# PEER gather on one Trainium2 core: remaining u dots and the first v-row gathers issued at the last u tile, v rows at a new pace

## The chip, the cores and the metric

The kernel runs on 1 core of one Trainium2 chip. The metric is device time in microseconds (us) of one execution. Before the change the median of 3 runs is 1949.45 us (1948.42 to 1951.34).

## What is computed

Two decoder layers over 256 tokens with 1024 channels, then a final RMS norm. Each layer is a token mixer (attention) and then PEER, a feed-forward layer that looks up experts. The change touches PEER alone. Per token it does this, for 8 heads with 16 chosen experts each out of 16384:

```python
q = (ht @ wq).reshape(PEER_CHUNK, PEER_HEADS, 2, half)
...
act = jax.nn.gelu(jnp.einsum('td,thkd->thk', ht, u[e]))
return jnp.einsum('thk,thkd->td', gate * act, v[e])
```

`e` are the numbers of the chosen experts (top-k of two half keys), `gate` a softmax over their scores. `u` and `v` are tables of 16384 rows of 1024 float32 values (64 MB each) per layer.

## The kernel before

The 256 tokens of a layer are split. The first ND = 160 tokens are computed **densely**: `u` is walked in NI = 128 tiles of 128 experts, each tile multiplied with all 160 tokens (L1444), put through GELU on ScalarE (L1432) and kept in SBUF as `A` (128 experts x 160 tokens per tile). The gates are then spread into `A` by one-hot products, and `v` is walked in 128 tiles of 128 rows that are multiplied with `A` and summed in four PSUM banks (L1506). The other 96 tokens (`PARTS`: 64 tokens with 2 slots each, 32 with 4) are computed by **gathering**: GpSimd issues indirect DMAs (L1215) that fetch 128 rows of `u` or `v` each, one row per partition, 96 for `u` and 96 for `v` per layer (`LOTS`). A gather of u rows is used by one dot on VectorE (`dot`, L1236); when all 96 dots are there, ScalarE applies GELU to them (`weigh`, L1240) and VectorE multiplies the gates in (`gated`, L1243). A gather of v rows is used by one scaled addition on VectorE (`axpy`, L1250 and L1252; two sums, `side` for the 64 tokens, `rows` for the 32).

The stages of a layer's PEER, on TensorE (PE): query products; 128 u tiles (L1420 to L1445); the one-hot stage of 40 steps of four tokens (`tb`, L1456 to L1475), where GpSimd makes one and VectorE three of four one-hots (L1409), ScalarE the other side (L1398, L1404), PE the gate products (`spread_gates`, L1416) and VectorE multiplies them into `A` (L1475); 128 v tiles (L1498 to L1522). Four tiles before the end, `gathered_part` (L1485) folds the two sums of gathered rows into the tokens by products with a stacking matrix: first half `side` (L1491, 128x64), second half `rows` (L1491, 128x32). The last three v tiles follow it on PE.

What sets the order. The program is written in one order by the Python loops, and every engine works through its own part of it in that order. A gather needs a free room (1024 columns): five in `side`, two in `rows`, and three more (`htok`, `junk`) once `gated` is issued. `pump()` issues gathers for the rooms that are free; `step(n)` calls it, uses row set n and gives its room back. `gather()` takes the next of the generator's steps (dots, `weigh`, `gated`, additions) if it may run, and the credit says how many steps a tile issues: 0.8 per u tile (`FETCH_PACE`), and per v tile `V_PACE` = (0.7 up to tile 106, then 1.2):

```python
credit[0] = min(credit[0] + V_PACE[0 if i < V_PACE[1] else 2], 2.0)
if credit[0] > 0 and head(gathers) is not None and i < NI - 9:
    nc.vector.tensor_copy(seen, ahead[max(ahead)][:, 0:1])
while credit[0] > 0 and gather():
    credit[0] -= 1
```

The `seen` copy (L1510) makes VectorE wait for the newest v tile that has been asked for before the steps of the tile run, so that the next gather goes out only after it. At tile 122 (`NI - GE`) all steps that are left are issued. The v tiles are loaded from SP's queue (`feed`, L387) into ten pieces (the first twelve at step 2 of the one-hot stage: six pieces, four places in `flat`, two in `spare`), gathers go over GpSimd's queue. In layer 0 the next layer's first weights are loaded at tile 119 (L1560) and split at tiles 122, 125 and 126 (`CUTS`, L395 on ScalarE, L397 on VectorE).

Of the kernel before, what the change touches and what calls it, by code (L numbers as in the profile page):

```python
# [28 lines left out]
NI = 128  # L29
# [29 lines left out]
GP = 4  # L59
HAND = 9  # L60
CUTS = {NI - 6: 1, NI - 3: 2, NI - 2: 3}
V_PACE = (0.7, 106, 1.2)
BG = (1, 0.7)
N0 = 2
C01 = 0
# [51 lines left out]
class Build:  # L117
# [1080 lines left out]
    def gather_steps(self, l, Q, more):  # L1198

        nc = self.nc  # L1200
        col = lambda i: Q[:, 1024 * i:1024 * (i + 1)]
        free = [col(i) for i in (0, 1, 2, 3, 7)] + more[2:]
        junk = col(6)
        htok, acc = [col(4), more[0]], [col(5), more[1]]
        dots = self.dots
        box = []

        open_to = lambda n: n < len(todo) and todo[n][3] <= self.rows

        def pump():  # L1210
            n = len(box)
            while free and open_to(n):
                table, lot = todo[n][0], todo[n][1]
                r = free.pop(0)
                nc.gpsimd.indirect_dma_start(out=r, out_offset=None, in_=self.a[table],  # L1215
                                             in_offset=bass.IndirectOffsetOnAxis(ap=self.gidx[:, lot:lot + 1], axis=0))
                box.append(r)
                n += 1

        starts = [SEQ - sum(n for n, _ in PARTS[:a + 1]) for a in range(len(PARTS))]  # L1220

        def join(a):
            n, per = PARTS[a]
            h2 = junk.rearrange("p (k s t) -> p k s t", k=KC, s=per)
            for k in range(KC):
                nc.vector.tensor_copy(h2[:, k], self.whole[:, k, None, starts[a]:starts[a] + n].to_broadcast([128, per, n]))

        def tokens(a, half):
            p = self.bank()
            for j in range(4):  # L1230
                k = 4 * half + j
                nc.tensor.transpose(p[:, j * 128:(j + 1) * 128], junk[:, k * 128:(k + 1) * 128], self.ident)  # L1232
            nc.scalar.activation(htok[a][:, half * 512:half * 512 + 512], p, AF.Copy)

        def dot(n, lot, a):
            nc.vector.scalar_tensor_tensor(junk, box[n], 1.0, htok[a], op0=OP.mult, op1=OP.mult,  # L1236
                                           accum_out=dots[:, lot:lot + 1])

        def weigh():
            nc.scalar.activation(dots, dots, AF.Gelu_apprx_tanh)  # L1240

        def gated():
            nc.vector.tensor_mul(dots, dots, self.ggate)  # L1243

        begun = set()

        def axpy(n, lot, a):
            if a not in begun:
                begun.add(a)
                nc.vector.tensor_scalar(acc[a], box[n], dots[:, lot:lot + 1], None, op0=OP.mult)  # L1250
            else:
                nc.vector.scalar_tensor_tensor(acc[a], box[n], dots[:, lot:lot + 1], acc[a], op0=OP.mult, op1=OP.add)  # L1252

        lots = []
        for heads in (4, 8):
            at = 0
            for a, (n, per) in enumerate(PARTS):
                w = 64 // per
                lots += [(at + (heads // 4 - 1) * w + i, a, heads) for i in range(w)]
                at += 128 // per  # L1260
        todo = [("u", lot, dot, heads, a) for lot, a, heads in lots] + [("v", lot, axpy, 8, a) for lot, a, heads in lots]

        def step(n):
            pump()
            todo[n][2](n, todo[n][1], todo[n][4])
            free.append(box[n])

        self.gacc = acc
        self.pump = pump
        for a in range(len(PARTS)):  # L1270
            for f in (lambda a=a: join(a), lambda a=a: tokens(a, 0), lambda a=a: tokens(a, 1)):
                yield (lambda: True), f
        for n in range(len(todo)):
            if n == LOTS:
                yield (lambda: self.routed[1]), weigh
                yield (lambda: self.routed[1]), gated
                free += [*htok, junk]
            yield (lambda n=n: n < len(box) or bool(free) and open_to(n)), lambda n=n: step(n)

    def peer(self, l, want, pos, early, then):  # L1280
# [12 lines left out]
        gathers = iter(())  # L1293
        self.pump = lambda: None
        heads = {}
        credit = [0.0]
        self.tv = self.tp = self.now = 0.0
        self.rows = self.q_done = 0
        self.asked, self.routed, self.coded = [False, False], [False, False], [False, False]
        END = (0.0, None, None)  # L1300

        def head(x):
            if x not in heads:
                heads[x] = next(x, None)
            return heads[x]
# [17 lines left out]
        def finish():  # L1323
            while route(True):
                pass
            assert all(self.routed)

        def gather():
            s = head(gathers)
            if s is None or not s[0]():  # L1330
                return False
            del heads[gathers]
            self.dve(1.2)
            s[1]()
            return True

        def fill(pace, most):
            if self.rows:
                credit[0] = min(credit[0] + pace, 3.0)
            while self.tv < self.now + most:  # L1340
                if credit[0] > 0 and gather():
                    credit[0] -= 1
                elif not route():
                    break
# [30 lines left out]
        gathers = self.gather_steps(l, G, [more[n // 2][:, n % 2] for n in range(4)])  # L1375
# [44 lines left out]
        for i in range(NI + 1):  # L1420
            if i == NI - 1:
                diffs = [self.bank() for _ in range(ND_)]
                for n in range(ND_):
                    differences(n)
            if i == NI:
                ohs = [self.piece(F32).rearrange("p (a n) -> p a n", a=8) for _ in range(NOH)]
                gates = [self.bank() for _ in range(NGB)]
                begin(0)
                begin(1)
                oh = [one_hots(n, False) for n in range(2)]  # L1430
            if i:
                nc.scalar.activation(dst(i - 1), ps.pop(i - 1)[:, :ND], AF.Gelu_apprx_tanh)  # L1432
            if i < NI:
                self.now += T_U
                if i == QROW:
                    finish()
                w = v(want(u0 + i, most=DEEP))
                for n, (b, after) in tiles.items():
                    if after >= 0 and after + 1 == i:
                        early[u0 + n] = ring[b]  # L1440
                        nc.sync.dma_start(ring[b], self.a["uT"][l, n])
                p = ps[i] = self.bank()
                for k in range(KC):
                    nc.tensor.matmul(p[:, :ND], w[:, k], self.whole[:, k, :ND], start=(k == 0), stop=(k == KC - 1))  # L1444
                fill(FETCH_PACE[0], SLACK)  # L1445
            else:
                first = spread_gates(0)
        vsrc = [self.a["v"][(l * NI + i) * 128:(l * NI + i + 1) * 128] for i in range(NI)]
# [7 lines left out]
        for tb in range(nb):  # L1456
# [5 lines left out]
            if tb == 2:  # L1462
                want(0, -1, most=PIECES - NOH)
                for n in range(4):
                    i = PIECES - NOH + n
                    ahead[i] = flat[:, NI * ND + n * UNIT:NI * ND + (n + 1) * UNIT]
                    nc.sync.dma_start(ahead[i], vsrc[i])
                for n in range(2):
                    i = PIECES - NOH + 4 + n
# [28 lines left out]
        for i in range(NI):  # L1498
            if i == NI - HAND:
                then([*[flat[:, NI * ND + n * UNIT:][:, :UNIT] for n in range(4)],  # L1500
                      *[spare[:, n * UNIT:(n + 1) * UNIT] for n in range(2)]])
            if l + 1 < DEPTH and i in CUTS:
                self.next[0](0, CUTS[i], most=0)
            r = want(i, most=DEEP if i < NI - 8 else 4)
            for k in range(KC):
                nc.tensor.matmul(acc[k], r[:, k * 128:(k + 1) * 128], dst(i), start=i == 0 and k % 2 == 0, stop=i == NI - 1,  # L1506
                                 skip_group_check=True)
            credit[0] = min(credit[0] + V_PACE[0 if i < V_PACE[1] else 2], 2.0)
            if credit[0] > 0 and head(gathers) is not None and i < NI - 9:
                nc.vector.tensor_copy(seen, ahead[max(ahead)][:, 0:1])  # L1510
            while credit[0] > 0 and gather():
                credit[0] -= 1
            if i == NI - GE:
                while gather():
                    pass
            if i == NI - GP:
                gathered_part()
            if i == NI - 2:
                for k in range(KC):
                    self.sum_chunk(squares[:, k], ND, SEQ, k)  # L1520
            if i == NI - SQ:
                self.load_sqrt()  # L1522
# [137 lines left out]
```

## Time and profile before

| | |
|---|---|
| median of 3 runs | 1949.45 us (1948.42 to 1951.34) |
| the profiled execution | 1956.64 us, its span 1954.8 us |
| TensorE (PE) busy | 1857.3 us, 95% |
| weight loads (PEld) | 1779.2 us, 91% |
| VectorE (DVE) | 1288.4 us, 66% |
| ScalarE (ACT) | 500.4 us, 26% |
| GpSimd (POOL) | 573.4 us, 29% |
| DMA | 605.26 MB, mean 310 GB/s; SP's queue 401.71 MB, GpSimd's 201.35 MB |
| granted TensorE clock, mean | 0.971 of full speed |

The profile is of one execution, a few us longer than the median of the runs. An engine's share is an average over stages with different limits, so the stages are read one by one: by the groups of instructions (what ended the idle time ahead of them), by the timeline of an engine in a stretch, and by the busy time and traffic of stretches. [...]

### The profile page before, as it was taken

How to read it: one execution, taken by the hardware profiler on the slowest of the kernel's cores; microseconds unless marked ns; L12 is line 12 of the kernel's file. 1: busy time of each engine (PE TensorE's matmuls, PEld its weight loads, DVE VectorE, ACT ScalarE, POOL GpSimd, SP SyncE). 2: the span in 40 equal slices, each digit the busy share in tenths (PEclk: the TensorE clock that was granted, in tenths of full speed). 3: DMA queues.
4: the chain of work that ended last, by engine and by line, in shares of the span. 5: the costliest groups of instructions: out<-in, count | busy, mean ns of one | idle time of the engine just before them, and what ended most of it. 6: DMA issues, size and time to landing. Idle time of an engine off the chain costs nothing. (4 is left out here: it accounts for less than half of the span.)

```text
span 1954.8 us, 34450 instructions
## 1 busy us (share of the span) xinstructions
PE 1857.3 (95%) x13284; PEld 1779.2 (91%) x13284; DVE 1288.4 (66%) x3084; ACT 500.4 (26%) x1079; POOL 573.4 (29%) x524
## 2 busy tenths in 40 slices
PE   5899999999999999999879999999999999999996
PEld 4778898999999899999868799899999998999995
DVE  8788765789854854444765987578995458344456
ACT  3444545211211710000025554522111154000001
POOL 4000005245443533322400000243454344322341
PEclk7899999999999999999989999999999999999997
DMA  7767656899999379999926574589999974999993
GB/s 274 282 229 261 218 162 240 325 386 365 409 408 409 140 270 375 409 409 408 407 96 240 204 267 163 200 294 366 366 409 408 409 295 145 349 408 408 407 410 155
DMA packets 166484, 605.26 MB, mean 310 GB/s; under 512 B 18480, under 2 KB 19120, under 8 KB 166192
## 3 DMA queue, kind: packets, MB, share of 16 engines
q1 hardware_dynamic: 111024, 401.71, 54.8%
q0 software_dynamic: 55296, 201.35, 26.3%
q8 instruction: 105, 1.72, 0.4%
q14 instruction: 59, 0.48, 0.1%
HBM read 601.94 MB, written 1.05 MB: 308 GB/s over the span
## 5 line engine op out<-in xcount | busy, mean ns | idle before, releaser
L1506 PE MATMUL bank<-wide,piece 128*128 128x160 f32 x3904 | 535.8, 300 | 2.6 <-DVE wide L1475 2.6
L1506 PEld LDWEIGHTS bank<-wide,piece 128*128 128x128 f32 x3904 | 534.4, 191 | 3.0 <-DVE wide L1475 3.0
L1444 PE MATMUL bank<-whole,piece 128*128 128x160 f32 x2624 | 360.7, 299 | 0.7 <-issue 0.4
L1444 PEld LDWEIGHTS bank<-whole,piece 128*128 128x128 f32 x2624 | 357.5, 190 | 1.6 <-issue 1.6
L1215 POOL DMA_INDIRECT side<-in_u_dram,routes x140 | 164.1, 1172 | 263.5 <-DVE side L1236 161.6
L397 POOL TENSOR_TENSOR piece<-piece 128x1024 fp32r<-128x1024 f32 x28 | 68.2, 2442 | 530.3 <-ACT piece L395 526.9
L1510 DVE COPY seen<-piece 128x1 f32<-128x1 f32 x176 | 27.0, 153 | 294.1 <-DMA piece<-in_v_dram 285.8
L1215 POOL DMA_INDIRECT side<-in_v_dram,routes x134 | 135.3, 1010 | 281.2 <-DVE side L1252 170.1
L1444 PE MATMUL bank<-whole,wide 128*128 128x160 f32 x1472 | 205.5, 299 | 3.1 <-issue 3.1
L1444 PEld LDWEIGHTS bank<-whole,wide 128*128 128x128 f32 x1472 | 201.3, 190 | 3.6 <-issue 3.4
L1432 ACT ACTIVATE wide<-bank 128x160 f32<-128x160 f32 x256 | 77.7, 305 | 469.3 <-PE bank L1444 406.0
L420 PE MATMUL bank<-hHL,piece 128*128 128x256 f32 (+1 forms) x592 | 176.7, 299 | 17.5 <-ACT hHL L344 14.2
L421 PE MATMUL bank<-hHL,piece 128*128 128x256 f32 (+1 forms) x592 | 174.9, 295 | 5.5 <-POOL hHL L347 4.3
L422 PE MATMUL bank<-hHL,piece 128*128 128x256 f32 (+1 forms) x592 | 173.5, 293 | 4.5 <-DVE piece L397 3.4
L395 ACT ACTIVATE piece<-piece 128x1024 fp32r<-128x1024 f32 x140 | 146.3, 1062 | 98.6 <-issue 37.3
L397 DVE TENSOR_TENSOR piece<-piece 128x1024 fp32r<-128x1024 f32 (+1 forms) x112 | 138.3, 1240 | 49.5 <-ACT piece L395 43.3
L1236 DVE SCALAR_TENSOR_TENSOR side<-side 128x1024 f32<-128x1024 f32 x94 | 114.9, 1222 | 45.0 <-DMA side<-in_u_dram,routes 35.1
L420 PEld LDWEIGHTS bank<-hHL,piece 128*128 128x128 f32 (+1 forms) x592 | 117.5, 199 | 20.4 <-ACT hHL L344 15.1
L421 PEld LDWEIGHTS bank<-hHL,piece 128*128 128x128 f32 (+1 forms) x592 | 117.2, 198 | 9.4 <-POOL hHL L347 6.4
L422 PEld LDWEIGHTS bank<-hHL,piece 128*128 128x128 f32 (+1 forms) x592 | 117.5, 199 | 6.5 <-DVE piece L397 4.9
L1252 DVE SCALAR_TENSOR_TENSOR side<-side,routes 128x1024 f32<-128x1024 f32 x86 | 110.5, 1285 | 0.4 <-DMA side<-in_v_dram,routes 0.3
L261 DVE SCALAR_TENSOR_TENSOR wide<-wide 128x1024 f32<-128x1024 f32 x80 | 97.7, 1222 | 16.9 <-DMA wide<-in_w_ada_dram 16.9
(244 smaller groups left out, 2777.8 us busy)
## 6 DMA issues: line engine op xcount, KB each, us to landing
piece<-in_v_dram SPq DMA_DIRECT2D x244, 512.0 KB
piece<-in_uT_dram SPq DMA_DIRECT2D x164, 512.0 KB
piece<-in_W_dram SPq DMA_DIRECT2D x147, 512.0 KB
wide<-in_uT_dram SPq DMA_DIRECT2D x92, 512.0 KB
wide<-in_w_ada_dram SPq DMA_DIRECT2D x80, 512.0 KB
side<-in_w_ada_dram SPq DMA_DIRECT2D x16, 512.0 KB
wide<-in_v_dram SPq DMA_DIRECT2D x8, 512.0 KB
side<-in_u_dram,routes POOLq DMA_INDIRECT x140
```

The lines of the kernel that those rows point to most:

```text
L261: nc.vector.scalar_tensor_tensor(buf(n), buf(n), 1.0, self.S["silu"], op0=OP.mult, op1=OP.mult, accum_out=self.mod[l][:, u:u + 1])
L395: nc.scalar.activation(Hs[i], raws[i], AF.Copy)
L397: self.subs.append(lambda: eng.tensor_sub(Ls[i], raws[i], Hs[i].bitcast(F32)))
L420: mm(out, l[0], r[0], start=start, stop=False, skip_group_check=True)
L421: mm(out, l[0], r[1], start=False, stop=False, skip_group_check=True)
L422: mm(out, l[1], r[0], start=False, stop=stop, skip_group_check=True)
L1215: nc.gpsimd.indirect_dma_start(out=r, out_offset=None, in_=self.a[table], in_offset=bass.IndirectOffsetOnAxis(ap=self.gidx[:, lot:lot + 1] ...
L1236: nc.vector.scalar_tensor_tensor(junk, box[n], 1.0, htok[a], op0=OP.mult, op1=OP.mult, accum_out=dots[:, lot:lot + 1])
L1252: nc.vector.scalar_tensor_tensor(acc[a], box[n], dots[:, lot:lot + 1], acc[a], op0=OP.mult, op1=OP.add)
L1432: nc.scalar.activation(dst(i - 1), ps.pop(i - 1)[:, :ND], AF.Gelu_apprx_tanh)
L1444: nc.tensor.matmul(p[:, :ND], w[:, k], self.whole[:, k, :ND], start=(k == 0), stop=(k == KC - 1))
L1506: nc.tensor.matmul(acc[k], r[:, k * 128:(k + 1) * 128], dst(i), start=i == 0 and k % 2 == 0, stop=i == NI - 1, skip_group_check=True)
```

## The change

Three things. At the last u tile (`i == NI - 1`) all dots that are left, `weigh` and `gated` are issued, and then `pump()` is called, so that v rows are gathered into every free room ahead of the one-hot stage (`self.weighed` counts the two steps). `V_PACE` becomes (1.25 for 8 tiles, then 0.74). The `seen` copy is left out in the first 8 v tiles.

```diff
-V_PACE = (0.7, 106, 1.2)
+V_PACE = (1.25, 8, 0.74)
...
         def weigh():
             nc.scalar.activation(dots, dots, AF.Gelu_apprx_tanh)
+            self.weighed = 1
 
         def gated():
             nc.vector.tensor_mul(dots, dots, self.ggate)
+            self.weighed = 2
...
-        self.rows = self.q_done = 0
+        self.rows = self.q_done = self.weighed = 0
...
                 fill(FETCH_PACE[0], SLACK)
+                if i == NI - 1:
+                    while self.weighed < 2 and gather():
+                        pass
+                    head(gathers)
+                    self.pump()
...
-            if credit[0] > 0 and head(gathers) is not None and i < NI - 9:
+            if credit[0] > 0 and head(gathers) is not None and V_PACE[1] <= i < NI - 9:
                 nc.vector.tensor_copy(seen, ahead[max(ahead)][:, 0:1])
```

How it moves instructions, at three places (both layers have the same). Line numbers behind the change are higher: its L1411 is L1409 of before (a one-hot), L1482 is L1475, L1244 is L1243 (`gated`), L1254 is L1252 (an addition), L1489 is L1482 (the tokens' sums).

GpSimd, from the last gathers of u rows to the first gathers of the v stage, as a difference (`piece` is a one-hot, `side` and `rows` the rooms):

```order
 L1215 DMA side<-in_u_dram,routes 128x1024 x5
-L1215 DMA rows<-in_v_dram,routes 128x1024
-L1409 TENSOR_SCALAR piece<-cst,routes 128x128 x5
-L1215 DMA rows<-in_v_dram,routes 128x1024
-L1409 TENSOR_SCALAR piece<-cst,routes 128x128 x35
+L1215 DMA rows<-in_v_dram,routes 128x1024 x2
 L1215 DMA side<-in_v_dram,routes 128x1024 x6
 L1215 DMA rows<-in_v_dram,routes 128x1024
 L1215 DMA side<-in_v_dram,routes 128x1024
+L1411 TENSOR_SCALAR piece<-cst,routes 128x128 x40
```

Ten gathers of v rows stand ahead of the 40 one-hots, where one stood ahead of them and one behind the fifth.

VectorE at the end of the u stage of layer 0. Before:

```order
L1236 SCALAR_TENSOR_TENSOR side,routes<-side,rows 128x1024 x5
L1236 SCALAR_TENSOR_TENSOR side,routes<-rows 128x1024 x2
L1409 TENSOR_SCALAR piece<-cst,routes 128x128 x9
L1475 TENSOR_TENSOR wide<-wide,bank 128x128x4
```

With the change:

```order
L1236 SCALAR_TENSOR_TENSOR side,routes<-side,rows 128x1024 x5
L1236 SCALAR_TENSOR_TENSOR side,routes<-rows 128x1024 x2
L1236 SCALAR_TENSOR_TENSOR side,routes<-side,rows 128x1024 x5
L1244 TENSOR_TENSOR routes<-routes 128x96
L1411 TENSOR_SCALAR piece<-cst,routes 128x128 x9
L1482 TENSOR_TENSOR wide<-wide,bank 128x128x4
```

Five dots and `gated` stand ahead of the first nine one-hots; before, they stood among the first v tiles.

VectorE at the end of the v stage of layer 0, from the last `seen` copy. Before:

```order
L1510 COPY seen<-piece 128x1
L1252 SCALAR_TENSOR_TENSOR rows<-side,routes,rows 128x1024 x5
L397 TENSOR_TENSOR piece<-wide,piece 128x1024 x2
L1252 SCALAR_TENSOR_TENSOR rows<-side,routes,rows 128x1024
L1252 SCALAR_TENSOR_TENSOR rows<-rows,routes 128x1024
L1252 SCALAR_TENSOR_TENSOR rows<-side,routes,rows 128x1024
L1252 SCALAR_TENSOR_TENSOR rows<-rows,routes 128x1024 x2
L1252 SCALAR_TENSOR_TENSOR rows<-side,routes,rows 128x1024 x4
L1482 SCALAR_TENSOR_TENSOR xT<-bank,mod_75,xT 128x64 x8
```

With the change:

```order
L1517 COPY seen<-piece 128x1
L1254 SCALAR_TENSOR_TENSOR rows<-rows,routes 128x1024
L1254 SCALAR_TENSOR_TENSOR rows<-side,routes,rows 128x1024 x3
L397 TENSOR_TENSOR piece<-wide,piece 128x1024 x2
L1254 SCALAR_TENSOR_TENSOR rows<-side,routes,rows 128x1024
L1489 SCALAR_TENSOR_TENSOR xT<-bank,mod_75,xT 128x64 x8
```

Five additions stand behind the last `seen` copy where fourteen stood, one of them behind the splits of the next layer's weights, where nine stood. In layer 1 there are no splits, and five and fourteen additions.

## Rows read from the trace of the kernel before

**Rows 1.** The page, busy time, share of the span and instructions of an engine.

```profile
PE 1857.3 (95%) x13284; PEld 1779.2 (91%) x13284; DVE 1288.4 (66%) x3084; ACT 500.4 (26%) x1079; POOL 573.4 (29%) x524
```

**Rows 2.** Groups by shape: count | busy us, mean ns | idle before, releaser.

```profile
L1506 PE MATMUL bank<-wide,piece 128*128 128x160 f32 x3904 | 535.8, 300 | 2.6 <-DVE wide L1475 2.6
...
L1491 PE MATMUL bank<-cst,rows 128*128 128x32 f32 x32 | 7.2, 401 | 27.5 <-DVE rows L1252 27.5
```

**Rows 3.** PE's timeline, layer 0's v stage: start us, us, what [idle before].

```profile
718.40 4.51 PE L1506 MATMUL bank<-wide,whole 128*128 128x160 f32 x32
...
968.33 1.89 PE L1491 MATMUL bank<-cst,side 128*128 128x64 f32 x16
986.49 3.60 PE L1491 MATMUL bank<-cst,rows 128*128 128x32 f32 x16 [16.27 <-DVE rows L1252]
989.90 6.55 PE L1506 MATMUL bank<-wide,piece 128*128 128x160 f32 x32
```

**Rows 4.** PE's timeline, the end of layer 1's v stage.

```profile
1915.76 1.89 PE L1491 MATMUL bank<-cst,side 128*128 128x64 f32 x16
1928.85 3.60 PE L1491 MATMUL bank<-cst,rows 128*128 128x32 f32 x16 [11.19 <-DVE rows L1252]
1932.26 6.42 PE L1506 MATMUL bank<-wide,piece 128*128 128x160 f32 x32
```

**Rows 5.** Stretches: us, busy of PE, PEld, DVE, ACT, POOL; PEclk, DMA, GB/s.

```profile
660.00:680.00 20.00, 20.00 (x133) 17.57 (x133) 20.00 (x59) 16.44 (x30) 12.38 (x15) 1.00 0.00 1
...
850.00:900.00 50.00, 50.00 (x370) 50.00 (x369) 22.11 (x33) 0.00 (x0) 15.03 (x16) 1.00 1.03 409
...
950.00:970.00 20.00, 20.00 (x153) 20.00 (x151) 14.38 (x17) 2.12 (x2) 11.29 (x10) 1.00 1.03 409
970.00:990.00 20.00, 3.73 (x19) 3.62 (x18) 15.53 (x20) 0.00 (x0) 1.02 (x1) 0.59 0.64 252
```

**Rows 6.** VectorE's timeline, the ends of the v stages of layers 0 and 1.

```profile
961.01 0.15 DVE L1510 COPY seen<-piece 128x1 f32<-128x1 f32 x1 [1.16 <-issue]
...
963.57 0.15 DVE L1510 COPY seen<-piece 128x1 f32<-128x1 f32 x1 [1.17 <-DMA piece<-in_v_dram]
963.68 6.57 DVE L1252 SCALAR_TENSOR_TENSOR rows<-side,routes,rows 128x1024 f32<-128x1024 f32 x5
970.16 2.36 DVE L397 TENSOR_TENSOR piece<-wide,piece 128x1024 fp32r<-128x1024 f32 x2
...
985.06 1.28 DVE L1252 SCALAR_TENSOR_TENSOR rows<-side,routes,rows 128x1024 f32<-128x1024 f32 x1 [0.28 <-DMA side<-in_v_dram,routes]
...
1910.24 7.89 DVE L1252 SCALAR_TENSOR_TENSOR rows<-side,routes,rows 128x1024 f32<-128x1024 f32 x6
```

**Rows 7.** Stretches, additions of line 1252 alone: us, DVE busy (count); PEclk, DMA, GB/s.

```profile
697.00:760.00 63.00, 15.42 (x12) 1.00 0.93 342
...
697.00:970.00 273.00, 108.93 (x85) 1.00 1.00 392
```

**Rows 8.** Timelines around layer 0's last u tile: VectorE, ScalarE, PE, GpSimd.

```profile
621.27 1.23 DVE L1236 SCALAR_TENSOR_TENSOR side<-rows 128x1024 f32<-128x1024 f32 x1 [1.33 <-DMA rows<-in_u_dram,routes]
...
622.42 1.75 DVE L1409 TENSOR_SCALAR piece<-cst,routes 128x128 f32<-128x128 f32 x6
...
643.72 0.69 DVE L1475 TENSOR_TENSOR wide<-wide,bank 128x512 f32<-128x512 f32 x1 [17.74 <-PE bank L1416]
...
638.67 0.30 ACT L1432 ACTIVATE wide<-bank 128x160 f32<-128x160 f32 x1 [2.25 <-PE bank L1444]
...
710.54 0.28 ACT L1240 ACTIVATE routes<-routes 128x96 f32<-128x96 f32 x1 [19.09 <-DVE side L1236]
...
642.56 1.05 PE L1416 MATMUL bank<-piece 128*128 128x128 f32 x8
...
643.04 0.79 POOL L1409 TENSOR_SCALAR piece<-cst,routes 128x128 f32<-128x128 f32 x1 [15.04 <-PE bank L1416]
```

**Rows 9.** SP's loads by line, 690 to 1000 us: count, ns min/median/max, first and last start.

```profile
L387 SPq DMA_DIRECT2D piece<-in_v_dram x116: 327/328/430, 691.3 to 966.1; - x116
```

## The prediction

> **What bounds the kernel now.** I read the page first: TensorE (PE) is busy 95% of the span [rows 1], so time can only come from the stretches where it stands still or runs at the lower clock. The groups of instructions by shape tell where those are. The products with the v tiles (L1506) have 2.6 us of idle time ahead of 3,904 records, but the second half of `gathered_part` (L1491 with `rows` as input) has 27.5 us ahead of its 32, released by the adding up of gathered v rows on VectorE (L1252) [rows 2]. That is the largest wait of PE for another engine in either layer's FFN, and the timeline of PE puts it in two places. In layer 0 PE ends the first half at 970.22 (968.33 + 1.89) and starts the second at 986.49: 16.27 us idle [rows 3]. In layer 1 it ends at 1917.65 and starts at 1928.85: 11.19 us [rows 4].
>
> The wait has a tail. After it, 16 records of the second half take 3.60 us where the 16 of the first took 1.89, and two v tiles take 6.55 us, where two at full clock take 4.51 [rows 3]; in layer 1 they take 3.60 and 6.42 [rows 4]. [...] So a stall costs its own length and then 1.71 + 2.04 us in layer 0, and 1.71 + 1.91 us in layer 1.
>
> Why the rows are late. VectorE's timeline shows it differently in each layer. In layer 1, fourteen row additions run back to back from the last `seen` copy: 6 take 7.89 us, so 14 take 18.4, from 1910.24 to 1928.7 [rows 6]. In layer 0, fourteen are left from 963.68, with two splits of the next layer's weights (2.36 us) among them, and the last addition waits until 985.06 for its gather to land [rows 6]. Behind both stand the transfers. A v tile and a gather are 512 KB each, which is 1.28 us at the 409 GB/s of 850 to 900 [rows 5]. On PE the 115 v tiles from tile 10 (718.40) to the first half of `gathered_part` (968.33) take 2.173 us each [rows 3]. At 0.7 gathers per tile the queues want 1.7 x 1.28 = 2.18 us per tile, all there is; the late pace of 1.2 wants 2.82. And two idle stretches are never made up: 660 to 680, in the one-hot stage, moves 1 GB/s [rows 5], and 697 to 760 moves 342 GB/s with 12 row additions done [rows 7], so (1 - 342/409) x 63 = 10.3 us of transfer time are lost there.
>
> **The change, part by part** (per layer, layer 0's times).
>
> *The last five dots, early.* VectorE ends its dots at 622.5 and then stands idle for 17.74 us before its first gate product at 643.72 [rows 8]. Dots come 2.56 us apart, paced by landings (1.23 us of work and 1.33 us of waiting [rows 8]). Five more end near 622.5 + 5 x 2.56 = 635.3. They are moved, not added: at their old place, the head of the v stage, no PE work waited for them. Cost 0, covered by VectorE's idle time; without that cover they would cost 5 x 1.3 = 6.5 us per layer.
>
> *Weighing ahead of the one-hots.* It stands on ScalarE behind the activation at 638.67 and takes 0.28 us [rows 8], so it ends near 639.3; `gated` follows to about 639.8. Behind it on VectorE wait nine one-hots that ran from 622.4: 1.75 us for 6 [rows 8], so 2.6 us for all, to 642.4. PE's first gate product at 642.56 [rows 8] needs only the first three of them (640.7), and the first product on VectorE was at 643.72. On ScalarE the step before the one-hots moves by 0.3 us at most. Cost 0 to 1.
>
> *Gathers ahead of GpSimd's one-hots.* GpSimd now issues ten v gathers before its first one-hot, where it issued one, then five one-hots, then another. Six go out while the dots run; four follow the last dot at about 0.95 + 0.3 us each, so GpSimd is free near 635.5 + 5 = 640.5 and its one-hot (0.79 us [rows 8]) is done before 642.56. The other bound is that each of the four waits for a landing at the shared rate, 4 x 2.56 = 10.2 us. I take 0.5 us per layer for the head as a whole: the rows around it show 17 us of slack, and it is nearest to those.
>
> *Eight gathers moved into the idle stretch.* Ten v gathers instead of two are issued before the gate products. The twelve v tiles loaded there plus eight gathers are 26 us of transfers, and 660 to 680 has next to none [rows 5]. Free for PE: no product needs them before 696. In the v stage 116 tile loads [rows 9] and 94 gathers become 116 and 86: 202 x 1.28 = 259 us instead of 269, against 125 tiles x 2.173 + 1.9 = 273.5 us of PE to the point where the rows must be ready.
>
> *Ten additions without a `seen` copy, then 0.74.* At 1.25 per tile for eight tiles ten additions run on VectorE at once (13 us), freeing ten rooms by about 710. The 10.3 us lost before 760 are recovered in part or in full. At 0.74 the queues want 1.74 x 1.28 = 2.23 us per tile, 0.057 more than PE takes: 5.9 us of lag over tiles 8 to 111. There the gathers end (the 96th goes out when the 86th addition frees its room) and the last 11 tiles want only 1.28 us each, so the lag is made up.
>
> *The end.* Layer 1 now has five additions behind the last `seen`: even if that copy came as late as now, 1910.2 + 5 x 1.31 = 1916.8, before the 1917.65 at which PE gets there. Residue 0. In layer 0 four additions, the two splits and one addition stand there: 963.7 + 5.3 + 2.4 + 1.3 = 972.7 at worst by that route, and by landings 985.06 - 10.3 = 974.8 with nothing of the lost time recovered, 964.5 with all, plus 1.3; PE arrives at 970.22. Residue 0 to 5.9 us; I take 1.5, nearer the recovered end because ten rooms come free at once.
>
> **Sum.** Waits 16.27 + 11.19 = 27.5; low clock 3.75 + 3.62 = 7.4; together 34.8. Given back: 1.5 in layer 0, 1.0 at the two heads. Net 32.3 us: the profiled execution would go from 1956.64 to 1924.3. Its time is 7.2 us over the median of the runs, 1949.45. If that difference stays, the median becomes 1917; if all of it lay in these waits, 1924. I take **1918 us**.
>
> Where the freed time goes next: PE runs through both halves and the last three tiles at full clock. The next thing that could be late is the squares of the gathered tokens, wanted two tiles (4.4 us) after the second half, and ready 2.3 us after it (1.36 us on VectorE, 0.85 on ScalarE). They fit.
>
> **A rule against the change.** The additions at the end of layer 0 come 2.56 us apart, each behind the `seen` copy of a new v tile (961.01, 963.57 [rows 6]): a v tile lands every 2.56 us, twice its 1.28 us, while both queues have work. [...]
>
> **The rivals.**
> *Rows still late.* The 5.9 us of lag and the next layer's weights on the same queue eat what was won. For it: 0.74 is over what the queues give. Against: 10.3 us are moved away for certain, and layer 1's end hangs on VectorE's 14 additions, not on landings. Half of the 34.8 stays: gain 17.4, 1932 (1922 to 1938). Chance 0.12.
> *The one-hot stage starts late.* GpSimd's four gathers wait for landings, 10.2 us per layer: 20.4 of the 34.8 back, net 14, 1935. For it: the twelve v tiles load at that time. Against: at most ten transfers stand ahead and VectorE has 17 us of slack. Chance 0.06.
> *It does not do what it says.* The `seen` copies hold the additions to the landing of tiles from tile 8 on, so the earlier start is lost by the end and the same stall returns: 1946 to 1953. Against: fewer additions are left behind the last copy whatever the copies do. Chance 0.05.
> *Slower: v tiles late.* With ten rooms free at once the gathers keep their queue full and a v tile lands every 2.56 us against 2.173 on PE. Eight tiles ahead are 17.4 us of cover; at 0.387 us per tile it is gone after 45 tiles in a row, and that is the point from which it decides. Over tiles 8 to 111 PE would wait 40 - 17.4 = 22.6 us per layer, 45 in all, less the 32 gained: +13, 1962. For it: the 2.56 us above. Against: L1506 has no wait for a transfer now, though the queues have been full from 760 to 970 [rows 2, 7], and each gather still goes out only after a v tile has landed. Chance 0.06.
>
> **How the numbers follow.** My forecast, both stalls gone or nearly so (1912 to 1924), has 0.71. Faster by over 0.2% (3.9 us, about what a measurement here can tell from no change) are the forecast and the first two rivals: 0.89; same is the third, 0.05; slower the fourth, 0.06. Low end: all 34.8 gained and some 3 us of scatter, 1912. High end: two thirds of the first rival, 1934; that leaves out about 0.2.
>
> **What would show it.** Right: no idle time ahead of the second half of `gathered_part`, or under 6 us in layer 0; its 16 records near 1.9 us and the two tiles after it near 4.5; a granted clock of 1.00 to the end of the stage; over 20 additions done by 760; traffic in 660 to 680 no less and gathers ahead of the one-hots; PE's first gate product within 1 us of now, counted from the end of the last u tile. Wrong: PE idle for a v tile in the v stage, a gap before the first gate product over 2 us, or additions still waiting for landings when PE reaches the second half.

## The result and the profile after

| | before | changed |
|---|---|---|
| median (both on the same chip) | 1950.39 us (1948.42 to 1952.63, 4 runs) | 1921.66 us (1919.84 to 1925.21, 4 runs) |
| the profiled execution | 1956.64 us, span 1954.8 us | 1919.84 us, span 1918.1 us |
| TensorE (PE) busy | 1857.3 us, 95% | 1844.3 us, 96% |
| granted TensorE clock, mean | 0.971 | 0.986 |

The ratio is 0.9848, with a 95% interval of 0.983 to 0.9866: the change is faster by 1.5%, which is 29.6 us by the ratio; the two medians lie 28.7 us apart. The forecast was 1918 us (1912 to 1934).

PE's groups by shape, changed kernel (count | busy us, mean ns | idle before, releaser):

```profile
L1513 PE MATMUL bank<-wide,piece 128*128 128x160 f32 x3904 | 532.0, 299 | 2.6 <-DVE wide L1482 2.6
...
L1418 PE MATMUL bank<-piece 128*128 128x128 f32 x640 | 97.6, 289 | 2.5 <-POOL piece L1411 1.4
...
L1513 PE MATMUL bank<-wide 128*128 128x160 f32 x128 | 18.0, 299 | 1.1 <-issue 1.1
...
L1498 PE MATMUL bank<-cst,rows 128*128 128x32 f32 x32 | 3.8, 274 | 0.0
```

The last row answers to [rows 2]: 27.5 us of idle time have become 0.0, and a product takes 274 ns instead of 401. Two rows above it carry waits that the kernel before did not have: 1.4 us for GpSimd's one-hot and 1.1 us at a v tile.

PE's timeline at the end of the v stage, layer 0 and layer 1, against [rows 3, 4]:

```profile
967.36 1.89 PE L1498 MATMUL bank<-cst,side 128*128 128x64 f32 x16
969.09 1.92 PE L1498 MATMUL bank<-cst,rows 128*128 128x32 f32 x16
970.85 4.59 PE L1513 MATMUL bank<-wide,piece 128*128 128x160 f32 x32
...
1894.19 1.90 PE L1498 MATMUL bank<-cst,side 128*128 128x64 f32 x16
1895.92 1.92 PE L1498 MATMUL bank<-cst,rows 128*128 128x32 f32 x16
1897.68 4.59 PE L1513 MATMUL bank<-wide,piece 128*128 128x160 f32 x32
```

The second half follows the first without a gap, and the granted clock is 1.00 from 967.4 to 975.4 and from 1894.2 to 1902.2; in the kernel before it was 0.50 in the second half of either layer, and 0.69 and 0.71 over the two tiles behind it. VectorE's timeline shows why the gap is gone (last `seen` copy, the additions behind it, layer 0 and layer 1), against [rows 6]:

```profile
956.91 0.14 DVE L1517 COPY seen<-piece 128x1 f32<-128x1 f32 x1
957.03 1.28 DVE L1254 SCALAR_TENSOR_TENSOR rows<-rows,routes 128x1024 f32<-128x1024 f32 x1
958.35 3.93 DVE L1254 SCALAR_TENSOR_TENSOR rows<-side,routes,rows 128x1024 f32<-128x1024 f32 x3
962.19 2.35 DVE L397 TENSOR_TENSOR piece<-wide,piece 128x1024 fp32r<-128x1024 f32 x2
964.46 1.28 DVE L1254 SCALAR_TENSOR_TENSOR rows<-side,routes,rows 128x1024 f32<-128x1024 f32 x1
...
1886.10 5.25 DVE L1254 SCALAR_TENSOR_TENSOR rows<-side,routes,rows 128x1024 f32<-128x1024 f32 x4
```

The last addition ends at 965.7 (964.46 + 1.28), 3.4 us before PE wants it; in layer 1 at 1891.35, 4.6 us before. No addition at the end waits for a landing any more. Additions alone by stretch (DVE busy and count; PEclk, DMA, GB/s), against [rows 7]:

```profile
697.00:760.00 63.00, 29.39 (x23) 1.00 0.96 369
697.00:970.00 273.00, 119.33 (x93) 1.00 1.00 393
```

23 additions are done by 760 where there were 12. All engines, against [rows 5]:

```profile
620.00:640.00 20.00, 18.56 (x118) 15.96 (x118) 9.12 (x22) 5.11 (x14) 8.72 (x10) 1.00 1.03 409
640.00:660.00 20.00, 19.24 (x141) 17.62 (x142) 17.97 (x52) 16.60 (x33) 16.27 (x20) 1.00 0.94 375
660.00:680.00 20.00, 20.00 (x134) 17.37 (x133) 20.00 (x59) 16.13 (x29) 12.40 (x15) 1.00 0.01 4
...
970.00:990.00 20.00, 18.61 (x136) 16.69 (x136) 14.36 (x42) 10.57 (x21) 4.68 (x5) 1.00 0.00 1
```

The first two stretches in the kernel before:

```profile
620.00:640.00 20.00, 19.82 (x138) 18.24 (x136) 3.90 (x11) 3.35 (x11) 5.48 (x5) 1.00 1.02 405
640.00:660.00 20.00, 20.00 (x148) 18.30 (x147) 16.27 (x47) 17.38 (x34) 13.06 (x15) 1.00 0.65 249
```

Where the stall was, the clock is 1.00 instead of 0.59. From 620 to 640 the transfers were full already (405 GB/s, now 409), so the early gathers share that stretch with the u tiles; 640 to 660 carries 375 GB/s where it carried 249. PE stands still for 1.4 and 0.8 us in the two, and 660 to 680 is as empty as before (4 GB/s).

Where the time went, stage by stage, from PE's first record of a stage to that of the next (us, before, changed, difference):

| stage | layer 0 | layer 1 |
|---|---|---|
| first u product to first gate product | 291.98, 294.14, +2.2 | 293.35, 292.84, -0.5 |
| one-hot stage | 54.00, 54.12, +0.1 | 54.00, 54.34, +0.3 |
| first v product to `gathered_part` | 271.77, 272.48, +0.7 | 271.77, 272.49, +0.7 |
| `gathered_part` to the end of the tokens' sums | 36.71, 16.68, -20.0 | 31.50, 16.68, -14.8 |

(The first row holds PE's wait for the first gate product too.) These make -31.3 us. The profiled executions differ by 36.8; the other 5.5 us lie in stages that the change does not touch, 4.0 of them ahead of layer 0's u tiles. That stretch runs the same code in all eleven traces (before, changed, and the nine runs below) and took 344.8 to 350.9 us (350.6 before, 346.6 changed), so this part is scatter between executions and not a gain. The first row scatters as well: in the six traces without early gathers layer 1 took 290.05 to 293.35, so its -0.5 says nothing. In layer 0 those six took 290.3 to 292.0 and the five with early gathers 292.7 to 294.1: a cost of some 2 us there is clear.

### The profile page after: what moved, and what is told of

It is laid out like the page before. It is cut to its first block, busy times and chain, and to the rows that moved or that the text cites. A ratio compares the mean times of both kernels' runs of the same rounds, so it can differ in the third digit from the quotient of the medians.

```text
span 1918.1 us, 34432 instructions
## 1 busy us (share of the span) xinstructions
PE 1844.3 (96%) x13284; PEld 1764.7 (92%) x13284; DVE 1286.7 (67%) x3072; ACT 500.2 (26%) x1079; POOL 566.3 (30%) x524
## 5 line engine op out<-in xcount | busy, mean ns | idle before, releaser
L1215 POOL DMA_INDIRECT side<-in_v_dram,routes x134 | 129.7, 968 | 231.2 <-DVE side L1254 113.0
L420 PE MATMUL bank<-hHL,piece 128*128 128x256 f32 (+1 forms) x592 | 175.2, 296 | 19.6 <-ACT hHL L344 15.5
L421 PE MATMUL bank<-hHL,piece 128*128 128x256 f32 (+1 forms) x592 | 172.9, 292 | 7.2 <-POOL hHL L347 6.1
L422 PE MATMUL bank<-hHL,piece 128*128 128x256 f32 (+1 forms) x592 | 171.6, 290 | 4.4 <-DVE piece L397 3.3
L420 PEld LDWEIGHTS bank<-hHL,piece 128*128 128x128 f32 (+1 forms) x592 | 115.5, 195 | 22.9 <-ACT hHL L344 16.8
L421 PEld LDWEIGHTS bank<-hHL,piece 128*128 128x128 f32 (+1 forms) x592 | 115.3, 195 | 11.2 <-POOL hHL L347 8.1
L422 PEld LDWEIGHTS bank<-hHL,piece 128*128 128x128 f32 (+1 forms) x592 | 115.6, 195 | 6.5 <-DVE piece L397 4.8
L1254 DVE SCALAR_TENSOR_TENSOR side<-side,routes 128x1024 f32<-128x1024 f32 x86 | 110.5, 1285 | 0.5
```

Of the source, the lines that this page charges most:

```text
L420: mm(out, l[0], r[0], start=start, stop=False, skip_group_check=True)
L421: mm(out, l[0], r[1], start=False, stop=False, skip_group_check=True)
L422: mm(out, l[1], r[0], start=False, stop=stop, skip_group_check=True)
```

## The experiments

**Each half alone.** `e1_early_old_pace` keeps the early dots and gathers and has the old pace and the old `seen` copies:

```diff
-V_PACE = (1.25, 8, 0.74)
+V_PACE = (0.7, 106, 1.2)
...
-            if ... and V_PACE[1] <= i < NI - 9:
+            if ... and i < NI - 9:
```

> The change with the old pace (0.7 per tile to tile 106, then 1.2) and a seen copy in every tile: only the early dots and the early gathers are left. Theory A (the gathers moved into the idle one-hot stage and the steps taken out of the v stage carry the gain): 7 additions stand behind the last seen copy in either layer instead of 14; with that copy 5.6 to 9.5 us ahead of gathered_part they end 0 to 2 us late in layer 1 and, with the two weight splits among them, 0 to 5 us late in layer 0. Idle time of PE ahead of the second half 0 to 7 us in all; 22 to 32 us under the kernel before. Theory B (the even pace carries it): idle of PE 18 us or more, gain under 12 us.

Measured: 1929.81 us (1928.16 to 1931.68), ratio 0.9895 (0.987 to 0.992), a gain of 20.5 us by the ratio, a little under the 22 to 32 of theory A and far above theory B. `e2_pace_only` is the kernel before with the new pace, and the copies left out in the first eight tiles, alone:

> The kernel before with the new pace (1.25 for 8 tiles, then 0.74) and no seen copy in the first 8 tiles, but dots, weighing and gathers where they were. Theory A: the five dots and two more steps still take their turns in the v stage, so 12 additions (15.8 us) stand behind the last seen copy; PE idle 4.6 to 8.5 us in layer 1 and 6 to 13 us in layer 0, low clock after both; gain 6 to 17 us. Theory B (the even pace carries it): idle under 4 us, gain 25 us or more.

Measured: 1942.84 us (1938.18 to 1944.71), ratio 0.9962 (0.9949 to 0.9976), a gain of 7.4 us, inside theory A's 6 to 17. The second half of `gathered_part` on PE's timeline, layer 0, first of the early half alone, then of the pace alone:

```profile
970.85 3.59 PE L1498 MATMUL bank<-cst,rows 128*128 128x32 f32 x16 [4.34 <-DVE rows L1254]
```

```profile
975.79 3.59 PE L1491 MATMUL bank<-cst,rows 128*128 128x32 f32 x16 [11.28 <-DVE rows L1252]
```

In layer 1 the waits are 1.97 and 8.32. So of 27.5 us of waiting the early half alone leaves 6.3, the pace alone 19.6, and both together 0. The gains, 20.5 and 7.4, make 27.9, which is nearly the whole. The early issue is the larger part.

**The `seen` copies.** `e3_seen_everywhere` is the changed kernel with the copies in the first eight v tiles too:

```diff
-            if ... and V_PACE[1] <= i < NI - 9:
+            if ... and i < NI - 9:
```

> The change with a seen copy in the first 8 v tiles as well. Theory A: in the change the last addition ends 3.4 us (layer 0) and 4.6 us (layer 1) before PE needs it, and the copies can only delay the first ten additions by some us, which the queues make up after tile 111; no idle time ahead of the second half, within 3 us of the change, 26 to 32 us under the kernel before. It also tells whether the 0.55 us in which PE stands still at v tile 7 belongs to ten gathers going out at once: then it is gone. Rival (leaving the copies out carries the start): PE idle over 5 us, gain under 24 us.

Measured: 1919.44 us (1915.45 to 1922.75), ratio 0.9839 (0.9809 to 0.9868): no different from the change. There is no idle time ahead of the second half, and the wait at the v tile is gone (a v stage of 271.77 us instead of 272.5). Leaving out the copies there was worth nothing. `e4_no_seen` has no `seen` copy at all:

```diff
-            if ... and V_PACE[1] <= i < NI - 9:
-                nc.vector.tensor_copy(seen, ahead[max(ahead)][:, 0:1])
```

> The change without any seen copy: the gathers keep their queue full. Theory A, with the rival 'v tiles late' put where it can act: a v tile lands every 2.56 us while both queues have work, against 2.173 on PE, until the 96th gather is out near tile 86; 86 x 0.387 = 33 us of lag less 17 us of tiles ahead, so PE waits some 16 us per layer for v tiles, and the time is 1940 to 1960, 20 to 40 us over the change. Other theory (the copies are not needed, the queue of v tiles holds its own): within 4 us of the change, no idle time of PE for v tiles.

Measured: 1952.0 us (1947.38 to 1958.22), ratio 1.0019 (1.0002 to 1.0035), some 33 us above the change by the ratios, inside the 20 to 40 expected. Its v tiles on PE, and its DMA queues from 730 to 900 us (packets, MB, share of 16 engines; then KB each and median us to landing):

```profile
L1513 PE MATMUL bank<-wide,piece 128*128 128x160 f32 x3904 | 554.1, 301 | 15.3 <-DMA piece<-in_v_dram 3.7 <-DVE wide L1482 2.6
```

```profile
q0 software_dynamic: 9514, 34.64, 51.1%
q1 hardware_dynamic: 9512, 34.65, 51.0%
...
piece<-in_v_dram SPq DMA_DIRECT2D x70, 512.0 KB, 20.4
```

Gathers and tiles share the engines evenly here (51.1% and 51.0%), 70 tiles are asked for in 170 us, one in 2.43 us where PE wants one in 2.17. The stage to `gathered_part` takes 289.1 us instead of 272.5 in layer 0. This is the prediction's slower rival, and what keeps it away in the change is the copy from tile 8 on.

**The clock.** `e5_busy_filler` is the kernel before with products of no use between the two halves:

```diff
+FILL = (70, 46)
...
+                if a:
+                    self.busy(FILL[l])
```

> The kernel before, with products of no use (70 in layer 0, 46 in layer 1, into a bank that nobody reads) put on PE between the two halves of gathered_part, so that it works through some 14.9 and 9.8 us of the two waits and the rows come no earlier. Theory A (the clock falls because PE stands still in the wait, and that is 7.4 us of the 34.8): the 16 records of the second half near 1.9 us instead of 3.6, the two v tiles after it near 4.5 instead of 6.5, time 5 to 8 us under the kernel before. Theory B (something else holds the clock down at that place, or a low clock costs nothing on the path): second half still 3.6 us, time within 3 us of the kernel before. If the products reach past the wait, they cost what they reach over: up to 3 us.

Measured: 1947.28 us (1945.07 to 1953.65), ratio 0.9974 (0.9959 to 0.9988), 5.1 us by the ratio. In layer 0, 0.48 us of standing still were left, the second half took 1.94 us and the tiles 4.59. In layer 1, 1.29 us were left, and the two took 2.72 and 7.16, which is read as a lower clock. So `e9_longer_filler` takes 72 and 53 products:

> As e5_busy_filler, with 72 and 53 products instead of 70 and 46, so that they reach to within 0.2 us of the rows in layer 0 and past them by up to 0.5 us in layer 1, where 1.29 us of standing still were left and the clock had fallen. Theory A (the clock falls because PE stands still): in layer 1 too the 16 records of the second half near 1.9 us and the two v tiles near 4.5; time 5 to 8 us under the kernel before, 0 to 4 us under e5_busy_filler. Theory B (the light products of the two halves and of the filler, and not the standing still, are what the clock falls after): layer 1 has a low clock again, second half over 2.5 us or the two v tiles over 6 us, time within 1.5 us of e5_busy_filler.

Measured: 1943.04 us (1940.69 to 1945.41), ratio 0.9968 (0.9955 to 0.9982), 6.2 us by the ratio. Layer 1 on PE's timeline, first of `e5_busy_filler`, then of `e9_longer_filler`, and last layer 0 of `e9_longer_filler`:

```profile
1917.50 2.72 PE L1494 MATMUL bank<-cst,rows 128*128 128x32 f32 x16 [1.29 <-DVE rows L1253]
1920.03 7.16 PE L1509 MATMUL bank<-wide,piece 128*128 128x160 f32 x32
```

```profile
1921.13 1.94 PE L1494 MATMUL bank<-cst,rows 128*128 128x32 f32 x16
1922.91 4.59 PE L1509 MATMUL bank<-wide,piece 128*128 128x160 f32 x32
...
984.80 1.94 PE L1494 MATMUL bank<-cst,rows 128*128 128x32 f32 x16 [0.98 <-DVE rows L1253]
```

The rows come no earlier, PE does more work, and the kernel is faster. The granted clock in `e9_longer_filler` is 1.00 in every stretch read, 964 to 990 and 1895 to 1930. So these two stalls cost their own length and the low clock behind them; that second part is worth 6.2 us here (3.5 to 8.8 by the interval) against 7.4 in the sum. The stages of `e9_longer_filler` from `gathered_part` on are 3.3 and 3.4 us shorter than before, 6.7 in all. How short a stall may be is not shown: behind 0.98 us in layer 0 the second half took 1.94 us, behind 1.29 us in `e5_busy_filler` 2.72, each in one execution.

**What the change gave back.** `e6_spread` holds the v gathers back until the one-hot stage and sends one every third step:

```diff
-            while free and open_to(n):
+            while free and open_to(n) and n < self.limit:
...
+        self.limit = LOTS
...
+            if tb >= 4 and tb % 3 == 1:
+                self.limit += 1
+                self.pump()
```

(After the one-hot stage the limit is lifted.)

> The changed kernel, but no gather of v rows goes out before step 4 of the one-hot stage; from there one every third step, the rest at the v stage. The five dots and the weighing stay at the last u tile, the pace stays. Theory A (what the change gave back are u tiles that land every 2.56 us beside the gathers, six of them in layer 0 and two in layer 1, and a wait of 1.4 us for GpSimd's one-hot behind its gathers): the last u tiles at 2.17 us, no wait of PE for GpSimd at the head, rows still in time at the end (no idle ahead of the second half), 3 to 5 us under the changed kernel. Theory B (the early gathers are needed as early as the change has them): idle comes back ahead of the second half, at least 4 us in layer 0, time the same as the change or above. Theory C (gathers between GpSimd's one-hots make these late): PE waits for GpSimd through the one-hot stage, 3 to 10 us per layer, time above the change.

`e7_spread_seen` adds the copies of `e3_seen_everywhere`:

> The kernel of e6_spread with the seen copy in the first eight v tiles too. Theory A: the 0.55 us that PE stands still at v tile 7 of each layer is gone, so 0 to 1.5 us under e6_spread; rows in time. Theory B (with the gathers spread, the copies now hold the first additions back far enough to be seen at the end): idle ahead of the second half in layer 0 and a time above e6_spread by over 2 us.

> The changed kernel itself, so that e6_spread and e7_spread_seen stand beside it on the same chip: 1917 to 1925, ratio to the kernel before 0.983 to 0.987.

Measured on one chip:

| | median us | ratio to before |
|---|---|---|
| `e8_change_again` | 1925.25 (1924.22 to 1929.27) | 0.9854 (0.9839 to 0.987) |
| `e6_spread` | 1922.75 (1922.14 to 1923.58) | 0.9843 (0.9829 to 0.9856) |
| `e7_spread_seen` | 1920.17 (1918.65 to 1922.04) | 0.9829 (0.9816 to 0.9843) |

The runs of `e7_spread_seen` and of the change do not overlap: 5.1 us between the medians, the best version here on one chip. `e6_spread` lies 2.5 us under the change, a little short of the 3 to 5 expected, and `e7_spread_seen` 2.6 us under `e6_spread`, above the 0 to 1.5 expected. Activations of late u tiles on ScalarE's timeline (one per tile, so the steps are the tiles' lengths), of the change and then of `e6_spread`:

```profile
622.52 0.30 ACT L1434 ACTIVATE wide<-bank 128x160 f32<-128x160 f32 x1 [2.23 <-PE bank L1446]
625.08 0.30 ACT L1434 ACTIVATE wide<-bank 128x160 f32<-128x160 f32 x1 [2.25 <-PE bank L1446]
...
632.76 0.30 ACT L1434 ACTIVATE wide<-bank 128x160 f32<-128x160 f32 x1 [2.26 <-PE bank L1446]
635.32 0.30 ACT L1434 ACTIVATE wide<-bank 128x160 f32<-128x160 f32 x1 [2.25 <-issue]
```

```profile
621.41 0.30 ACT L1435 ACTIVATE wide<-bank 128x160 f32<-128x160 f32 x1 [1.87 <-PE bank L1447]
623.58 0.30 ACT L1435 ACTIVATE wide<-bank 128x160 f32<-128x160 f32 x1 [1.87 <-PE bank L1447]
...
632.27 0.30 ACT L1435 ACTIVATE wide<-bank 128x160 f32<-128x160 f32 x1 [1.87 <-PE bank L1447]
634.57 0.30 ACT L1435 ACTIVATE wide<-bank 128x160 f32<-128x160 f32 x1 [1.99 <-PE bank L1447]
636.93 0.30 ACT L1435 ACTIVATE wide<-bank 128x160 f32<-128x160 f32 x1 [2.06 <-PE bank L1447]
```

In the change the last u tiles come 2.56 us apart, six in a row. With the gathers held back they come at 2.17, and the last two at 2.30 and 2.36. The change's second cost is at the head of the one-hot stage, on GpSimd's and PE's timelines:

```profile
638.90 0.95 POOL L1215 DMA_INDIRECT side<-in_v_dram,routes  x1 [2.00 <-issue]
639.89 10.44 POOL L1411 TENSOR_SCALAR piece<-cst,routes 128x128 f32<-128x128 f32 x12
...
640.76 1.16 PE L1418 MATMUL bank<-piece 128*128 128x128 f32 x8 [1.39 <-POOL piece L1411]
```

PE waits 1.39 us for the one-hot behind the tenth gather, which itself went out 2.00 us behind the end of the ninth; in the other four traces with early gathers PE's wait in layer 0 is 2.0 to 3.0 us (2.1 in `e8_change_again`), and in layer 1 of the five 0 to 1.9. With the gathers spread PE does not wait for GpSimd. Stage by stage, `e7_spread_seen` against `e8_change_again`: u stages 291.73 and 292.28 against 294.02 and 294.08; one-hot stages 55.28 and 55.60 against 55.76 and 54.22; v stages 271.77 twice against 272.49 and 272.46. Against this execution 4.1 us are won in the u stages and 1.4 in the v stages; in the one-hot stages 0.9 is lost on balance. But `e8_change_again` was profiled in its slowest run (1929.27), with the longest u stage of layer 1 in eleven traces; against the change's first profile the same sums are 3.0 and 1.4 won and 2.4 lost. How the 5.1 us of the medians divide is therefore not settled, beyond the 2.3 and 2.4 us of layer 0's u stage. The gathers in the one-hot stage have a price, on PE's groups and VectorE's and GpSimd's timelines of `e7_spread_seen`:

```profile
L1419 PE MATMUL bank<-piece 128*128 128x128 f32 x640 | 98.6, 291 | 2.6 <-DVE piece L1412 1.4
```

```profile
646.99 1.45 DVE L1412 TENSOR_SCALAR piece<-cst,routes 128x128 f32<-128x128 f32 x3
...
648.61 0.85 DVE L1412 TENSOR_SCALAR piece<-cst,routes 128x128 f32<-128x128 f32 x3
...
654.57 0.87 DVE L1412 TENSOR_SCALAR piece<-cst,routes 128x128 f32<-128x128 f32 x3
...
647.13 1.09 POOL L1215 DMA_INDIRECT rows<-in_v_dram,routes  x1 [0.17 <-DVE wide L1486]
...
654.80 1.03 POOL L1215 DMA_INDIRECT side<-in_v_dram,routes  x1 [0.17 <-DVE wide L1486]
```

PE's wait is for VectorE, not for GpSimd as theory C had it. Three one-hots on VectorE take 0.85 us without a gather's issue on GpSimd. Beside the first three issues of layer 0 they take 1.18, 1.45 (here beside 647.13 to 648.22) and 1.34, but beside the fourth (654.80) 0.87 and beside the fifth 0.84, so an issue alone does not slow them.

## Why the prediction was right, and where it was off

*The stall.* Right in place, price and releaser. The sum took 34.8 us from the two ends; the two tails are 20.0 + 14.8 = 34.8 us shorter. That both halves were needed, and that the early one is worth more, is shown by the two runs of a half; that the low clock belongs to the price, by the busy PE of `e9_longer_filler` (6.2 us).

*The residue in layer 0.* Taken at 1.5 us, measured 0, with 3.4 us to spare: the additions no longer wait for landings, as its lower bound had it (964.5 + 1.3; measured 965.7).

*The five dots, the weighing.* The dots come 2.56 us apart, as forecast, and end at 633.1 (the dots of this execution ran 2.2 us ahead of the one before); no PE work waits for them: cost 0, as forecast. One row was misread on the way: VectorE's 17.74 us of idle time lie behind its nine one-hots, from 625.98, and not right behind the dots at 622.5.

*Gathers ahead of GpSimd's one-hots.* Mis-sized. The step had GpSimd free 5.2 us behind the last dot and PE there 7.3 us behind it. GpSimd was free 6.75 us behind it (639.85), because the tenth gather went out 2.00 us behind the end of the ninth instead of 0.3, for what the profile does not name; PE was there 6.3 us behind it (639.37), and then waited 1.4 us for the one-hot. The 0.5 us taken for a layer is 1.4 to 3.0 in layer 0 and 0 to 1.9 in layer 1 over the five traces with early gathers.

*Eight gathers moved into the idle stretch, "Free for PE".* This step failed in its place, not in its gain. Most of the ten gathers run not in the empty stretch but ahead of it, beside the last u tiles, from 620 to 640 at 409 GB/s. Asked about products behind the u stage alone, the step overlooked the u tiles that still land. The last eight u tiles took 19.4 us (619.98 to 639.41 on ScalarE) where those of before took 17.8 (two of those were late already): 1.6 us. The rows of before:

```profile
624.97 0.31 ACT L1432 ACTIVATE wide<-bank 128x160 f32<-128x160 f32 x1 [1.87 <-PE bank L1444]
...
642.76 0.30 ACT L1432 ACTIVATE wide<-bank 128x160 f32<-128x160 f32 x1 [1.13 <-PE bank L1444]
```

A tile every 2.56 us while both queues have work was held against the change in the v stage; it came at the end of the u stage. From 620 to 640 GpSimd's queue moved 4.08 MB and SP's 4.07, and the u tiles came 2.56 us apart, twice the 1.28 us that 409 GB/s give for one alone.

*Ten additions without a copy.* 23 additions by 760, as forecast (over 20). But the missing copy was not the reason: with it the time is the same, and `e3_seen_everywhere` does 23 from 700 to 760. Without it PE stands still for some 0.55 us at a v tile in each layer.

*The rivals.* Rows late did not come about; the one-hot stage starts late by 1.4 (up to 3.0) of its 10.2 us. The slower one is real: without copies layer 0's v stage goes from 272.5 to 289.1 us, 16.6 more, where its working had 22.6 us per layer.

*The sum.* Given back by the rows above: 1.6 + 1.4 at layer 0's head and 0.7 in each v stage, 4.4 us, where 2.5 were taken; by the stages it is 3.5, and -31.3 stands against the forecast net of 32.3. Two misses partly cancel here, the residue (1.5 too much) and the heads (too little), which is luck. The 1918 also assumed that nearly all of the 7.2 us by which the profiled execution of before was above its median lay outside the stalls. There is one trace of that kernel, so this stays unchecked; the medians differ by 28.7 us, and the forecast had 31.5.

*The signs set down.* The main ones came: no idle time ahead of the second half, 1.92 us for its products and 4.59 us for the two tiles (6.27 in layer 0 of `e8_change_again`, see the last section), the clock at 1.00, over 20 additions by 760. One could not fail: 4 GB/s from 660 to 680 is "no less" than 1, though the gathers did not fill that stretch. Two signs of being wrong showed in small: PE stood still at a v tile (0.55 us), and the first gate product came 1.4 us behind the last u tile instead of within 1, and over 2 us behind it in `e8_change_again`. They are what was given back; the gain does not hang on them.

## What to carry to other kernels

When an engine waits at a stage's end for work that another could have begun earlier, look for the stretch in which the transfers rest, and start the work just inside it: what was started ahead of it here took bandwidth from loads that were wanted (u tiles 2.56 us apart instead of 2.17). Price a stall with the low clock behind it (6.2 us for the two stalls here, beside 27.5 us of waiting). A wait that looks like mere delay (a copy that holds a queue back to another's landings) may be what divides the bandwidth (without any copy the kernel was some 33 us slower); take it away alone and measure before it is left out.

## What was not expected of the hardware

The clock also fell where PE did not stand still, as read in `e7_spread_seen`. In layer 0 of `e3_seen_everywhere`, `e7_spread_seen` and `e8_change_again` the two tiles behind the second half took 6.27 us instead of 4.59, though PE had no gap; in the change's profile, in `e4_no_seen` and in `e6_spread` they took 4.59 (granted clock 1.00 in the change and in `e6_spread`). Stretches of `e7_spread_seen`:

```profile
967.90:969.70 1.80, 1.80 (x19) 1.80 (x18) 1.53 (x8) 0.00 (x0) 0.00 (x0) 1.00 0.00 0
969.70:972.00 2.30, 2.30 (x11) 2.30 (x11) 1.45 (x9) 0.68 (x1) 0.00 (x0) 0.54 0.00 0
```

PE is busy throughout, and the granted clock goes from 1.00 to 0.54 right behind the products of the two halves. Behind 1.29 us of standing still the two tiles took 7.16 us (`e5_busy_filler`), behind 0.98 us 4.59 (`e9_longer_filler`, layer 0), and here, behind none, 6.27, which is 1.7 us more; what decides it stays open. The first two are each a row of one execution.

And VectorE's one-hots grew slower beside the issue of some gathers on GpSimd (1.45 us for three instead of 0.85) and not beside others (0.87). No view tells what sets the two apart, so the cause stays open.
